# The weight-block sums for v's products: when their DRAM-to-DRAM transfers are asked for

## The chip, the core and the metric

The kernel runs on one core of a Trainium2 chip. A core has a matrix engine (TensorE, "PE" in the profile), a vector engine (VectorE, "DVE"), a scalar engine (ScalarE, "ACT"), GpSimd ("POOL"), SyncE ("SP"), and 16 DMA engines that all queues share. The metric is the device time of one execution in microseconds; a kernel's time is the median of its runs.

## What is computed

One decoder layer on x of shape (1, 512, 2048), in float32:

```python
h = _rmsnorm(x, g_pre)
proj = h @ w_in                                   # (512 x 2048) @ (2048 x 7168)
q, k, v, z_att, u, g_glu, z_conv = jnp.split(proj, IN_SPLITS, axis=-1)
y_att = _stick_breaking_attention(q, k, v) * jax.nn.silu(z_att)
y_conv = _conformer_conv(u, g_glu, conv_w, conv_b, ln_g, ln_b, w_pw2, b_pw2) * jax.nn.silu(z_conv)
y = jnp.concatenate([y_att, y_conv], axis=-1) @ w_out
return x + _rmsnorm(y, g_post)
```

Each of the seven parts of `proj` has 1024 columns. This case is about the part v, and about the parts u, q and k that are computed just before it.

## The kernel before

**Products.** Every float32 operand is split into a high and a low part, and a product takes three matrix multiplies (high by high, high by low, low by high). A weight block of 1 MB is loaded by one DMA that SP issues into a tile `r_...` (pool `raws`, two buffers); ACT makes the high part `h_...` from it (line 99, pool `his`, two buffers) and DVE the low part `l_...` (line 100, pool `los`, two buffers). So the load of one block waits until the split of the block two before it is through, and a high part is written only when PE has done the products with the high part two before it.

**The order of the work.** The opening (from line 1189) computes the first half of the gate g in sixteen blocks `(kg, m)` while x is loaded, transposed and normalised. Then the list `steps` is run (from line 1229). A step has one loaded weight block and two units of products; `n_v` = 6 steps come first (u, q and k for the first pair of heads: u0, u1, q0, q1, k0, k1 for short), and their units have 24 multiplies each. Then come the fourteen steps of `values()`, two for each of the seven products that v is made of, in the order 1, 2, 5, 6, 3, 7, 4. Their units have 12 multiplies each, so a block is needed twice as often there. They are called v10, v11, v20, v21, v50, v51 and so on: product, then half. Their tile is `r_v`, with the same name for all fourteen. PE's order is the program's; the order on DVE and ACT is fixed when the kernel is compiled. DVE also works through 240 steps of the convolution (`acc`, lines 396 and 401), placed between the others.

**The sums.** v is computed by a scheme with seven block products in place of eight; the weight operands of the products 5, 6, 7 and 4 are sums of blocks of `w_in`. These sums are made in DRAM by DMAs alone: for each sum and each of its two halves, a base block is copied into a DRAM tile `vs` (line 506), and then another block is added to it by an accumulating DMA (line 502). `plan_sums` (line 492) lists them in this order: copies of 5 (two halves), accumulations of 5, copies of 6 (from the finished sum 5, so `vs` to `vs`), accumulations of 6, copies of 7, accumulations of 7, copies of 4 (from sum 6), accumulations of 4. That is sixteen transfers of 1 MB each, all issued by GpSimd in this order. GpSimd also issues two loads of the opening and clears a small border tile `hg` (line 392).

**When a sum is asked for.** `sum_next` (line 514) takes the next transfer from the list and makes it wait for the last multiply that has been written down so far:

```python
def sum_next(todo):
    if todo:
        tc.add_manual_dep(
            todo.popleft()().ins, latest[0].name,
            ...
```

It is called with `v_sumq` at the end of each opening block from number 5 on (line 1197), and then after every unit of every step (line 1258), until the list is empty. Eleven transfers fall into the opening's blocks 5 to 15, and the other five wait for the first five units. A transfer that builds on another also waits for that one to land, and GpSimd issues in order. The halves of the sums are loaded by line 612 when the steps v50, v51, v60, v61, v70, v71, v40 and v41 come near.

The sums for the output projection (`ws`, `sumq`) are another list, asked for from step 18 on.

## Time and profile before

| | |
|---|---|
| median of 3 runs | 870.81 us (869.97 to 870.85) |
| the profiled execution: whole time | 871.51 us |
| the profiled execution: span from the first to the last instruction | 869.8 us |
| TensorE clock granted over it | 0.997 |
| DVE busy | 631.0 us (73%) |
| ACT busy | 395.3 us (45%) |
| GpSimd's DMA queue (q0): moved, share of the 16 engines' span | 52.43 MB, 26.1% |
| SP's DMA queue (q1): moved, share of the 16 engines' span | 110.12 MB, 37.3% |

The page of the profile gives shares over the whole span. What a transfer does to the work around it has to be read from narrow windows: the timeline of an engine gives start and length of each instruction, in brackets how long the engine sat idle before it and what ended that. The DMA share of a window is the mean busy share of the 16 DMA engines; it can go a little over 1, since packets overlap and are counted where they start.

### The profile page before, as it was taken

How to read it: one execution, taken by the hardware profiler on the slowest of the kernel's cores; microseconds unless marked ns; L12 is line 12 of the kernel's file. 1: busy time of each engine (PE TensorE's matmuls, PEld its weight loads, DVE VectorE, ACT ScalarE, POOL GpSimd, SP SyncE). 2: the span in 40 equal slices, each digit the busy share in tenths (PEclk: the TensorE clock that was granted, in tenths of full speed). 3: DMA queues.
4: the chain of work that ended last, by engine and by line, in shares of the span. 5: the costliest groups of instructions: out<-in, count | busy, mean ns of one | idle time of the engine just before them, and what ended most of it. 6: DMA issues, size and time to landing. Idle time of an engine off the chain costs nothing.

```text
span 869.8 us, 9834 instructions
## 1 busy us (share of the span) xinstructions
PE 855.0 (98%) x3894; PEld 710.0 (82%) x3894; DVE 631.0 (73%) x773; ACT 395.3 (45%) x452; POOL 124.5 (14%) x154
## 2 busy tenths in 40 slices
PE   9999998999999999999999999999999999999995
PEld 7888787888888888888888888888888888888884
DVE  4798799986797979879696984245643776458775
ACT  5785124644443544243422545235722346455542
POOL 0221100001202132203111323031001000000031
PEclk9999999999999999999999999999999999999998
DMA  8899964568578455874488547862232346556783
GB/s 324 250 272 283 281 158 160 185 207 302 173 181 174 165 193 145 179 189 165 145 192 165 176 157 183 175 162 97 93 101 97 98 154 233 194 194 250 289 279 101
DMA packets 87046, 163.58 MB, mean 188 GB/s; under 512 B 3014, under 2 KB 52434, under 8 KB 83224
## 3 DMA queue, kind: packets, MB, share of 16 engines
q1 hardware_dynamic: 69824, 110.12, 37.3%
q0 software_dynamic: 16864, 52.43, 26.1%
q8 instruction: 30, 0.49, 0.2%
q10 hardware_dynamic: 312, 0.40, 0.1%
q14 instruction: 16, 0.13, 0.0%
HBM read 158.75 MB, written 54.53 MB: 245 GB/s over the span
## 4 chain that ended last, share of the span: by engine, by line
PE 80%; DVE 10%; DMA 6%; ACT 2%; issue 1%; POOL 0%; DVEq 0%; ACTq 0%; POOLq 0%
PE za L342 3%; PE zc L342 3%; PE za L344 3%; PE a L940 3%; PE zc L344 3%; PE za L343 3%; PE a L942 3%; PE zc L343 3%; PE a L941 3%; DVE acc L401 3%; DVE l_v L100 3%; DMA r_k<-in_w_in_dram 3%; PE k L342 3%; PE q L344 3%; PE q L342 3%; PE u L344 3%
## 5 line engine op out<-in xcount | busy, mean ns | idle before, releaser
L401 DVE SCALAR_TENSOR_TENSOR acc<-hg,vec,acc 128x512 f32<-128x512 f32 x240 | 182.2, 759 | 6.8
L100 DVE TENSOR_TENSOR l_w<-r_w,h_w 128x2048 fp32r<-128x2048 f32 x28 | 64.1, 2291 | 41.9 <-ACT h_w L99 41.9
L99 ACT ACTIVATE h_w<-r_w 128x2048 fp32r<-128x2048 f32 x28 | 53.5, 1915 | 42.1 <-DMA r_w<-ws 11.8
L344 PE MATMUL k<-h_hi,l_k 128*128 128x512 f32 x128 | 50.1, 391 | 1.1 <-DVE l_k L100 1.1
L342 PE MATMUL u<-h_hi,h_u 128*128 128x512 f32 x128 | 50.3, 393 | 0.0
L342 PE MATMUL q<-h_hi,h_q 128*128 128x512 f32 x128 | 50.1, 392 | 0.0
L342 PE MATMUL k<-h_hi,h_k 128*128 128x512 f32 x128 | 50.0, 391 | 0.0
L342 PE MATMUL za<-h_hi,h_za 128*128 128x512 f32 x128 | 50.0, 390 | 0.0
L342 PE MATMUL zc<-h_hi,h_zc 128*128 128x512 f32 x128 | 49.9, 390 | 0.0
L344 PE MATMUL u<-h_hi,l_u 128*128 128x512 f32 x128 | 49.9, 390 | 0.0
L344 PE MATMUL q<-h_hi,l_q 128*128 128x512 f32 x128 | 49.9, 390 | 0.0
L344 PE MATMUL za<-h_hi,l_za 128*128 128x512 f32 x128 | 49.8, 389 | 0.0
L344 PE MATMUL zc<-h_hi,l_zc 128*128 128x512 f32 x128 | 49.8, 389 | 0.0
L343 PE MATMUL u<-h_lo,h_u 128*128 128x512 f32 x128 | 49.8, 389 | 0.0
L343 PE MATMUL k<-h_lo,h_k 128*128 128x512 f32 x128 | 49.8, 389 | 0.0
L343 PE MATMUL za<-h_lo,h_za 128*128 128x512 f32 x128 | 49.8, 389 | 0.0
L343 PE MATMUL q<-h_lo,h_q 128*128 128x512 f32 x128 | 49.8, 389 | 0.0
L343 PE MATMUL zc<-h_lo,h_zc 128*128 128x512 f32 x128 | 49.8, 389 | 0.0
L940 PE MATMUL a<-h_w,f_hi 128*128 128x512 f32 x128 | 49.8, 389 | 0.0
L941 PE MATMUL a<-l_w,f_hi 128*128 128x512 f32 x128 | 49.8, 389 | 0.0
L942 PE MATMUL a<-h_w,f_lo 128*128 128x512 f32 x128 | 49.8, 389 | 0.0
L671 POOL TENSOR_SCALAR_AFFINE_SELECT t<-t 128x128 f32<-128x128 f32 x64 | 35.7, 635 | 81.1 <-DVE t L694 48.2
(339 smaller groups left out, 2136.7 us busy)
## 6 DMA issues: line engine op xcount, KB each, us to landing
ws<-in_w_out_dram POOLq DMA_DIRECT2D x24, 1024.0 KB, 9.3
r_w<-ws SPq DMA_DIRECT2D x16, 1024.0 KB
vs<-in_w_in_dram POOLq DMA_DIRECT2D x12, 1024.0 KB, 12.9
r_w<-in_w_out_dram SPq DMA_DIRECT2D x12, 1024.0 KB
r_u<-in_w_in_dram SPq DMA_DIRECT2D x8, 1024.0 KB
r_q<-in_w_in_dram SPq DMA_DIRECT2D x8, 1024.0 KB
r_k<-in_w_in_dram SPq DMA_DIRECT2D x8, 1024.0 KB
r_v<-vs SPq DMA_DIRECT2D x8, 1024.0 KB
```

The lines of the kernel that those rows point to most:

```text
L99: nc.scalar.activation(hi, src, AF.Copy)
L100: nc.vector.tensor_tensor(out=lo, in0=src, in1=f32(hi), op=ALU.subtract)
L342: nc.tensor.matmul(ps, wh, ah, start=first, stop=False)
L343: nc.tensor.matmul(ps, wh, al, start=False, stop=False)
L344: latest[0] = nc.tensor.matmul(ps, wl, ah, start=False, stop=last).ins
L401: bgq.append(lambda j=j: nc.vector.scalar_tensor_tensor(out=acc, in0=hg[:, j : j + S], scalar=vec[:, ct, j : j + 1], in1=acc, op0=ALU.mult ...
L671: nc.gpsimd.affine_select(out=blk, in_=blk, compare_op=ALU.is_gt, fill=0.0, base=0, pattern=[[-1, P]], channel_multiplier=1,)
L940: nc.tensor.matmul(ps, fh[:, kk, ts], hi[:, k, :], start=st, stop=False, skip_group_check=True)
L941: nc.tensor.matmul(ps, fh[:, kk, ts], lo[:, k, :], start=False, stop=False, skip_group_check=True)
L942: nc.tensor.matmul(ps, fl[:, kk, ts], hi[:, k, :], start=False, stop=en, skip_group_check=True)
```

## The change

The first hunk moves the start of the requests in the opening from block 5 to block 10, so that six transfers (the copies and accumulations of sum 5, the copies of sum 6) are asked for there. The second hunk counts the units of the steps; after a unit a transfer is asked for only if the count isn't a multiple of three. The remaining ten transfers are so tied to the units 1, 2, 4, 5, 7, 8, 10, 11, 13 and 14, counted from the first unit of u0.

```diff
@@ -1194,7 +1194,7 @@
                 f()
             if n + 1 < len(blocks):
                 keeps[n + 1]()
-            if n >= 5:
+            if n >= 10:
                 sum_next(v_sumq)
...
+    units_done = 0
     for n, step in enumerate(steps):
...
         for unit in step.units:
             unit(w)
-            sum_next(v_sumq)
+            units_done += 1
+            if units_done % 3:
+                sum_next(v_sumq)
```

The list, its order, the transfers themselves and everything else stay as they are.

## The prediction

> **What bounds the kernel now.** First the page's busy times, then the waits of PE, which say whether anything but PE's own work is left.

> ```profile
> PE 855.0 (98%) x3894; PEld 710.0 (82%) x3894; DVE 631.0 (73%) x773; ACT 395.3 (45%) x452; POOL 124.5 (14%) x154
> ```

> ```profile
> PE va L635 <- DVE l_v L100: 2.4, 1, 2.4
> PE k L344 <- DVE l_k L100: 1.1, 1, 1.1
> PE va L634 <- ACT v_a L596: 0.4, 1, 0.4
> ```

> PE works for 98% of the span, and its own waits are few: 2.4 us at a block of v, 1.1 us at k, 0.4 us at a later block of v. The change can touch 1.1 + 2.4 = 3.5 us of this and no more: a faster delivery of weights can't shorten PE's own products. What it can add has no such limit.

> Where the two waits come from, in the chain of waits (start, length, what; in order of time):

> ```profile
> 58.12 19.88 DMA r_q<-in_w_in_dram
> 78.11 1.93 ACT h_q L99
> 80.06 2.30 DVE l_q L100
> 82.38 21.91 DMA r_k<-in_w_in_dram
> 104.39 1.93 ACT h_k L99
> 106.34 2.29 DVE l_k L100
> ```

> Two 1 MB loads in a row take 19.9 and 21.9 us; k0's low part is finished at 108.63. PE starts on it at once (the 1.1 us). DVE has been standing, and from here on it is late:

> ```profile
> 80.06 2.29 DVE L100 TENSOR_TENSOR l_q<-r_q,h_q 128x2048 fp32r<-128x2048 f32 x1 [3.88 <-ACT h_q L99]
> 92.50 9.40 DVE L401 SCALAR_TENSOR_TENSOR acc<-hg,vec,acc 128x512 f32<-128x512 f32 x12
> 106.34 2.29 DVE L100 TENSOR_TENSOR l_k<-r_k,h_k 128x2048 fp32r<-128x2048 f32 x1 [4.44 <-ACT h_k L99]
> 129.03 0.68 DVE L100 TENSOR_TENSOR k_lo<-k,k_hi 128x512 fp32r<-128x512 f32 x1
> 136.38 2.28 DVE L100 TENSOR_TENSOR l_v<-r_v,h_v 128x2048 fp32r<-128x2048 f32 x1
> 147.43 2.28 DVE L100 TENSOR_TENSOR l_v<-r_v,h_v 128x2048 fp32r<-128x2048 f32 x1
> ```

> It idles 3.88 us for q0 and 4.44 us for k0. No idle time stands before the later rows: DVE works without a gap from 106.34, so l_v of v11 (136.38) comes when its turn comes, ends at 138.66, and PE takes it up at 138.72:

> ```profile
> 68.73 0.50 PE L342 MATMUL u<-h_hi,h_u 128*128 128x512 f32 x1
> 130.48 0.39 PE L634 MATMUL va<-h_v,h_hi 128*128 128x512 f32 x1
> 138.72 0.50 PE L635 MATMUL va<-l_v,h_hi 128*128 128x512 f32 x1 [2.41 <-DVE l_v L100]
> 149.78 0.49 PE L635 MATMUL vc<-l_v,h_hi 128*128 128x512 f32 x1
> ```

> The last row is the first use of l_v of v21, which DVE ended at 147.43 + 2.28 = 149.71: the next block comes just in time, with no slack and no wait.

> Why the loads are slow: the DMA share of stretches (last two columns: share, GB/s).

> ```profile
> 61.00:101.00 40.00, 39.96 (x188) 32.88 (x186) 35.76 (x59) 15.35 (x20) 6.10 (x7) 1.00 1.07 285
> 121.00:200.00 79.00, 76.59 (x337) 62.66 (x336) 73.57 (x81) 39.06 (x40) 1.00 (x3) 1.00 0.51 174
> ```

> From 61 to 101 us the engines are full (1.07); after 121, when the sums have landed, they are half idle (0.51). That is what the change levels out. It matters that the half-idle stretch is the one where blocks are needed every 5.5 us instead of every 11.

> **The change, part by part.**

> *No instruction is removed or added on PE, DVE, ACT or SP.* The sixteen transfers stay; GpSimd only waits for other multiplies. Queued behind a waiting transfer on GpSimd are later transfers and the clearing of `hg` for u's next pair, which comes after the fourteen steps of v: free.

> *The new times.* From 68.73 (unit 2) to 130.48 (unit 13, v10) are 61.75 us, less the wait of 1.11, over eleven units: 5.51 us each. Without the waits, unit 4 ends at 85.3, 5 at 90.8, 7 at 101.8, 8 at 107.3, 10 at 118.3, 11 at 123.8, 12 at 129.4; units 13 and 14 are half as long and end at 132.1 and 134.8.

> The opening:

> ```profile
> 28.88 0.72 POOL L506 DMA_DIRECT2D vs<-in_w_in_dram  x1 [5.26 <-PE gn L478]
> 32.09 0.71 POOL L506 DMA_DIRECT2D vs<-in_w_in_dram  x1 [2.50 <-PE gn L478]
> DMA to landing us min/median/max: 5.5/5.6/5.7
> DMA to landing us min/median/max: 8.9/9.0/9.0
> L612 SPq DMA_DIRECT2D r_v<-vs x8: 319/330/349, 143.7 to 192.9; - x8
> ```

> Blocks are 3.2 us apart, so block 10 asks at 28.88 + 5 x 3.21 = 45 us. A copy alone lands in 5.6 us, an accumulation alone (here two of `ws`) in 9.0. Copies of 5 go out at 45 and 48, accumulations at 52 and 55; the copies of 6 wait for these to land (about 61 and 68), the accumulations of 6 for the copies (about 70 and 75), then units rule: copies of 7 at 85 and 91, accumulations of 7 at 102 and 107, copies of 4 at 118 and 124, **accumulations of 4 at 132.4 and 135.1**, landed by about 152. The eight halves are loaded from 143.7 to 192.9 us (last row) in the order 5, 6, 7, 4; sum 5 is there at 68, and by 143.7 all but sum 4, whose loads are the last two: no sum comes too late.

> *What goes: up to 3.5 us.* In flight while q0 loads (asked for at 58.12, which is set by DVE, not by a load) are two accumulations that are nearly done by 66 and two copies; before, two accumulations that had just started and three copies. I estimate q0 by 71 instead of 78. Its high part needs u0's buffer, free at unit 2's end (74.2), so the 3.9 us of idle DVE go. k0 is then asked for at about 78.5. From 72 to 100 the engines have two accumulations to move, three loads and two copies.

> ```profile
> q0 software_dynamic: 199, 0.41, 72.8%
> q1 hardware_dynamic: 174, 0.36, 35.5%
> q1 hardware_dynamic: 7, 0.01, 0.6%
> q1 hardware_dynamic: 481, 0.97, 94.2%
> ```

> Of the first two rows (112 to 115 us) an accumulation's packet takes 0.728 x 3 us x 16 / 199 = 0.176 us of one engine; 512 packets of 2 KB make 5.6 us of all sixteen. A load alone moves 481 packets in 3 us (last row), so 3.2 us. Two of the one, three of the other and two copies (under 5.6 each, I take 3) are 27 us of 28, with k0 ahead of the last ones: landed at about 92 to 95 instead of 104.3. It isn't wanted before its `h_k` buffer is free (unit 6, 96.3) and DVE's 12 convolution steps are over. So DVE's idle 4.44 us go as well. PE's 1.1 us go. For the 2.4 us, DVE must be ahead by 1.1 + 2.4 = 3.5 us at v11. What could hold it:

> ```profile
> 121.25 1.92 ACT L99 ACTIVATE h_v<-r_v 128x2048 fp32r<-128x2048 f32 x1 [9.97 <-DMA r_v<-in_w_in_dram]
> 125.24 0.60 ACT L99 ACTIVATE k_hi<-k 128x512 fp32r<-128x512 f32 x1 [2.08 <-PE k L344]
> 130.46 1.92 ACT L99 ACTIVATE h_v<-r_v 128x2048 fp32r<-128x2048 f32 x1 [4.61 <-PE k L343]
> 144.31 1.92 ACT L99 ACTIVATE h_v<-r_v 128x2048 fp32r<-128x2048 f32 x1 [2.13 <-PE va L636]
> ```

> k_hi (125.24) waits for unit 11, at 123.8 then and 124.9 before; right behind it comes k_lo on DVE, at 129.03 before, so DVE can be ahead by 4 us here. h_v of v11 (130.46) waits for PE, 1.1 us earlier. l_v of v11 then starts at about 132.2 and ends at 134.4; PE wants it at 135.0. Both waits go: **-3.5 us**. If only x of DVE's lead is kept, x goes (bounds 0 and -3.5).

> *What comes: v21's load among the accumulations of 4.* v21 is asked for when l_v of v11 frees its buffer: at 138.69 before, 134.4 then; the accumulations go out at 132.4 and 135.1, on both sides of it. Until now the loads of this stage met none. With both waits gone PE wants l_v of v21 at 149.78 - 3.51 = 146.3; behind the landing come 1.92 (h_v) and 2.28 (l_v), with 0.1 between. If v21 lands at L, the net change is L + 4.3 - 149.7 = **L - 145.4 us**, and never below -3.5 (L up to 141.9). Now L:

> ```profile
> 108.66 0.37 SPq L612 DMA_DIRECT2D r_v<-in_w_in_dram  x1
> 138.69 0.37 SPq L612 DMA_DIRECT2D r_v<-in_w_in_dram  x1
> 101.43 1.18 POOL L502 DMA_DIRECT2D vs<-in_w_in_dram  x1 [16.18 <-DMA vs<-vs]
> 104.33 1.16 POOL L502 DMA_DIRECT2D vs<-in_w_in_dram  x1 [1.72 <-DMA vs<-vs]
> DMA to landing us min/median/max: 11.7/14.2/16.6
> ```

> - From below: v21 before, without company, was asked for at 138.69 and used at 144.31, 5.6 us later, and ACT waited for PE there, not for it. L = 134.4 + 5.6 = 140.0: no new wait, net -3.5.
> - The nearest row: v10, the same kind of load, asked for at 108.66 beside two accumulations (101.43, 104.33) and landed when ACT took it at 121.25: 12.6 us. L = 147.0, net +1.6. Built from packets it is the same: hardly one has moved by 111 (7 packets in the 107 to 111 row), then 174 in 3 us; 512 take 8.8 us, so 2.9 + 8.8 and the tail.
> - From above: both accumulations go wholly ahead. The later of two landed 16.6 us after its issue: 135.1 + 16.6 = 151.7, net +6.3.

> I take 12.6 us, the row that is the same transfer in the same company. Afterwards nothing catches up: v50's load queues right behind and is needed 5.5 us later, and from then on PE stands as close behind DVE as before.

> Sum: -1.1 - 2.4 + 5.1 = **+1.6 us**. The profiled execution, 869.8 of span and 1.7 around it, becomes 871.5 + 1.6 = 873.1; its time is 0.7 above the median of the runs, so the forecast is 870.8 + 1.6 = **872.4 us**.

> [...]

> **The rivals.**

> - [...] 14%.
> - *v21 is hidden*: it gets through before the accumulations are dense, L below 141.9, full gain of 3.5: **867.3**. For it: 2 us pass between the issue of an accumulation and its flow. Against: the second is already queued. 22%.
> - *Slower: the accumulations win.* Place: v21, on the DMA queues from 132 to 152 us; price up to +6.3 (**877**); it decides from L = 147.1, as net +1.7 is the border. For it: the load at 82.38 took 21.9 us. 14%.
> - *The change does not do what it says*: q0 and k0 are no faster, for there are four accumulations and four copies between 52 and 101 as before; the waits stay, and v21, asked for late, meets less: about **870.8**. Against: q0 and k0 are met by other ones, older or lighter. 8%.

> The forecast has 42%, net +0.3 to +3.3.

> **How the numbers follow.** A measurement of this kernel can tell about 0.2% (1.7 us) from nothing. Faster: the second rival, 22%. Within 0.2%: the first and the last, and half the forecast's band, 43%. Slower: the other half and the third, 35%. The range reaches from the full gain, 867.3, to 875.8 (L = 150.4), leaving out the far end of the third rival and little below. The forecast's own band is 871.1 to 874.1.

> **What would show it.** Right: no wait of PE at k; q0 and k0 landing 7 to 10 us earlier; DVE without its two gaps; a new wait at v21 (vc, lines 634 and 635) of about 5 us, with the accumulations of 4 in flight over it. Wrong: no wait there (second rival); v21 asked for at another time than 134, which means that DVE's order or lead came out differently; a wait at v11 that stays.

## The result and the profile after

The changed kernel is **slower by 0.48%**: a median of 874.84 us (874.03 to 876.01, six runs) against 871.33 us (869.97 to 873.05, six runs) for the kernel before in the same comparison, a ratio of 1.0048 with a 95% interval of 1.0030 to 1.0065. The profiled execution took 874.75 us with a span of 873.0; before it took 871.51 with a span of 869.8. The forecast was 872.4, so the sign was right and the size, 1.6 us against 3.2 in the two profiled executions and 3.5 between the medians, was half of what came: 874.84 lies above the forecast's own band (871.1 to 874.1) and inside its range (up to 875.8).

The page's busy times after the change:

```profile
PE 856.5 (98%) x3894; PEld 712.0 (82%) x3894; DVE 631.1 (72%) x773; ACT 395.3 (45%) x452; POOL 124.6 (14%) x154
```

The instructions are as many as before. PE is busy for 1.5 us more (856.5 against 855.0) with the same multiplies, so some of them took longer; the span is 3.2 us longer, so the other 1.7 us are idle time. The waits of PE say where the idle time is:

```profile
PE vc L634 <- ACT h_v L99: 3.7, 1, 3.7
PE vc L635 <- DVE l_v L100: 1.8, 1, 1.8
```

The waits at k (1.1), at v11 (2.4) and at a later block (0.4) are gone. One new place has come, the first two multiplies of v21, with 3.7 and 1.8 us. The chain of waits around it (start, length, what):

```profile
131.18 2.30 DVE l_v L100
133.49 13.08 DMA r_v<-in_w_in_dram
146.67 1.92 ACT h_v L99
148.62 2.30 DVE l_v L100
150.96 0.79 PE vc L635
```

The low part of v11 ends at 133.46 and frees the buffer; v21 is asked for at once, lands at 146.57 after 13.08 us, and goes through ACT and DVE with PE standing still. GpSimd's issues in that stretch, on its timeline, and the landing line of the view of the sums' tile `vs` from 131 to 152 us:

```profile
131.61 1.19 POOL L502 DMA_DIRECT2D vs<-in_w_in_dram  x1 [7.64 <-PE va L636]
134.33 1.16 POOL L502 DMA_DIRECT2D vs<-in_w_in_dram  x1 [1.53 <-PE va L636]
```

```profile
DMA to landing us min/median/max: 10.1/13.4/16.7
```

The accumulations of sum 4 are issued at 131.61 and 134.33, on both sides of v21's request at 133.49, and land after 10.1 and 16.7 us, the second one at 151.0. The queues show how v21 got through between them: from 133.5 to 137.5 us (first two rows: packets, MB, share of the 16 engines' span; q0 is GpSimd's, q1 is SP's) and from 138 to 144 us (last two):

```profile
q0 software_dynamic: 297, 0.61, 104.6%
q1 hardware_dynamic: 3, 0.01, 0.5%
```

```profile
q0 software_dynamic: 395, 0.78, 69.6%
q1 hardware_dynamic: 392, 0.80, 39.8%
```

For 4 us the load moves three packets against 297; then the two queues move about as many packets, 395 against 392. This is the late start that the row of v10 had shown in the kernel before. About 1 us of it is there without company too: v21 in the kernel before, asked for at 138.69 with no accumulation in flight, moved its first packet between 139.70 and 139.75, 1.0 us after its request; here it took 3.8.

The other side of the ledger, on the timelines of ACT and of DVE (in brackets: idle time before, and what ended it):

```profile
74.05 1.92 ACT L99 ACTIVATE h_q<-r_q 128x2048 fp32r<-128x2048 f32 x1 [0.51 <-PE u L343]
97.90 1.92 ACT L99 ACTIVATE h_k<-r_k 128x2048 fp32r<-128x2048 f32 x1 [10.99 <-DMA r_k<-in_w_in_dram]
```

```profile
76.00 2.29 DVE L100 TENSOR_TENSOR l_q<-r_q,h_q 128x2048 fp32r<-128x2048 f32 x1
99.85 2.29 DVE L100 TENSOR_TENSOR l_k<-r_k,h_k 128x2048 fp32r<-128x2048 f32 x1 [1.29 <-ACT h_k L99]
131.18 2.28 DVE L100 TENSOR_TENSOR l_v<-r_v,h_v 128x2048 fp32r<-128x2048 f32 x1
148.62 2.29 DVE L100 TENSOR_TENSOR l_v<-r_v,h_v 128x2048 fp32r<-128x2048 f32 x1 [6.30 <-ACT h_v L99]
```

DVE's gap of 3.88 us at q0 is gone (the row at 76.00 has no bracket), and that at k0 has shrunk from 4.44 to 1.29. ACT takes q0 at 74.05 not when it lands but when PE frees the buffer. DVE reaches l_v of v11 at 131.18 instead of 136.38. So the early half of the change does what its diff says. What it doesn't explain is in PE's timeline behind the new wait:

```profile
148.64 0.50 PE L634 MATMUL vc<-h_v,h_hi 128*128 128x512 f32 x1 [3.73 <-ACT h_v L99]
150.96 0.79 PE L635 MATMUL vc<-l_v,h_hi 128*128 128x512 f32 x1 [1.82 <-DVE l_v L100]
151.55 0.63 PE L636 MATMUL vc<-h_v,h_lo 128*128 128x512 f32 x1
151.98 0.63 PE L634 MATMUL vc<-h_v,h_hi 128*128 128x512 f32 x1
...
156.67 0.40 PE L636 MATMUL vc<-h_v,h_lo 128*128 128x512 f32 x1
156.91 0.40 PE L634 MATMUL vc<-h_v,h_hi 128*128 128x512 f32 x1
```

Between 151.55 and 156.67 a multiply starts every 0.43 us and takes 0.63; then they are back at 0.23 and 0.40. The clock granted to PE is the last column but two in the view by windows:

```profile
146.00:148.60 2.60, 0.00 (x0) 0.00 (x0) 0.00 (x0) 1.93 (x2) 0.00 (x0) 1.00 1.05 343
148.70:150.90 2.20, 0.44 (x1) 0.12 (x1) 2.20 (x2) 1.64 (x4) 0.00 (x0) 0.76 0.72 174
151.00:156.00 5.00, 5.00 (x12) 3.94 (x13) 5.00 (x6) 2.62 (x3) 0.00 (x0) 0.50 0.59 210
156.90:160.00 3.10, 3.10 (x15) 2.54 (x14) 1.89 (x4) 0.81 (x1) 0.00 (x0) 1.00 0.88 307
```

The clock is 1.00 while PE waits for the high part, falls in the middle of the second wait (0.76 over that window), stands at **0.50 over the window from 151 to 156**, and is 1.00 again in the last one. Comparing the start of every multiply with the same multiply before gives the whole ledger, after minus before: -0.33 from the opening, -1.57 once k's wait is gone, -1.90 (a stall of 0.33 at k1 gone, too short for the list of waits), -4.63 at v11, +1.19 at the first multiply with l_v of v21 (149.78 before, 150.96 now), +3.84 at the end of the slow stretch, and about +3.2 from the next small wait (0.4 us, gone) to the end. What went and the two new waits together come to +1.2; the slow clock adds 2.65, more than twice that.

### The profile page after: what moved, and what is told of

It reads as the page before. It is cut to its first block, busy times and chain, and to the rows that moved or that the text cites. A ratio compares the mean times of both kernels' runs of the same rounds, so it can differ in the third digit from the quotient of the medians.

```text
span 873.0 us, 9834 instructions
## 1 busy us (share of the span) xinstructions
PE 856.5 (98%) x3894; PEld 712.0 (82%) x3894; DVE 631.1 (72%) x773; ACT 395.3 (45%) x452; POOL 124.6 (14%) x154
## 4 chain that ended last, share of the span: by engine, by line
PE 93%; DVE 3%; DMA 1%; ACT 1%; issue 0%; POOL 0%; DVEq 0%; ACTq 0%; POOLq 0%
PE u L342 3%; PE u L344 3%; PE za L342 3%; PE q L342 3%; PE q L344 3%; PE u L343 3%; PE zc L342 3%; PE za L344 3%; PE a L940 3%; PE zc L343 3%; PE zc L344 3%; PE q L343 3%; PE za L343 3%; PE a L941 3%; PE a L942 3%; PE k L342 3%
## 5 line engine op out<-in xcount | busy, mean ns | idle before, releaser
L401 DVE SCALAR_TENSOR_TENSOR acc<-hg,vec,acc 128x512 f32<-128x512 f32 x240 | 182.2, 759 | 6.8
L100 DVE TENSOR_TENSOR l_w<-r_w,h_w 128x2048 fp32r<-128x2048 f32 x28 | 64.1, 2291 | 42.1 <-ACT h_w L99 42.1
L99 ACT ACTIVATE h_w<-r_w 128x2048 fp32r<-128x2048 f32 x28 | 53.5, 1915 | 43.7 <-DMA r_w<-ws 16.1
L342 PE MATMUL u<-h_hi,h_u 128*128 128x512 f32 x128 | 50.3, 393 | 0.0
L342 PE MATMUL q<-h_hi,h_q 128*128 128x512 f32 x128 | 50.1, 392 | 0.0
L342 PE MATMUL k<-h_hi,h_k 128*128 128x512 f32 x128 | 50.0, 391 | 0.0
L342 PE MATMUL za<-h_hi,h_za 128*128 128x512 f32 x128 | 50.0, 390 | 0.0
L342 PE MATMUL zc<-h_hi,h_zc 128*128 128x512 f32 x128 | 49.9, 390 | 0.0
L344 PE MATMUL u<-h_hi,l_u 128*128 128x512 f32 x128 | 49.9, 390 | 0.0
L344 PE MATMUL q<-h_hi,l_q 128*128 128x512 f32 x128 | 49.9, 390 | 0.0
L344 PE MATMUL zc<-h_hi,l_zc 128*128 128x512 f32 x128 | 49.8, 389 | 0.0
L344 PE MATMUL za<-h_hi,l_za 128*128 128x512 f32 x128 | 49.8, 389 | 0.0
L343 PE MATMUL u<-h_lo,h_u 128*128 128x512 f32 x128 | 49.8, 389 | 0.0
L343 PE MATMUL za<-h_lo,h_za 128*128 128x512 f32 x128 | 49.8, 389 | 0.0
L344 PE MATMUL k<-h_hi,l_k 128*128 128x512 f32 x128 | 49.8, 389 | 0.0
L343 PE MATMUL q<-h_lo,h_q 128*128 128x512 f32 x128 | 49.8, 389 | 0.0
L343 PE MATMUL k<-h_lo,h_k 128*128 128x512 f32 x128 | 49.8, 389 | 0.0
L343 PE MATMUL zc<-h_lo,h_zc 128*128 128x512 f32 x128 | 49.8, 389 | 0.0
```

What stands on the lines that cost most here:

```text
L99: nc.scalar.activation(hi, src, AF.Copy)
L100: nc.vector.tensor_tensor(out=lo, in0=src, in1=f32(hi), op=ALU.subtract)
L342: nc.tensor.matmul(ps, wh, ah, start=first, stop=False)
L343: nc.tensor.matmul(ps, wh, al, start=False, stop=False)
L344: latest[0] = nc.tensor.matmul(ps, wl, ah, start=False, stop=last).ins
L401: bgq.append(lambda j=j: nc.vector.scalar_tensor_tensor(out=acc, in0=hg[:, j : j + S], scalar=vec[:, ct, j : j + 1], in1=acc, op0=ALU.mult ...
```

## The experiments

The theory after the result: the late start (first hunk) is a gain of about 3 us; the thinning (second hunk), on top of it, brings the last two accumulations beside v21's load; PE's wait there costs 5.5 us; and because of the wait, not because of the transfers, the clock falls and costs 2.65 more. The rivals: that the thinning is what unloads the opening, that v21 is late for another reason than these two accumulations, and that the slow multiplies come from the traffic of the DMAs.

### The first hunk alone

```diff
-            if n >= 5:
+            if n >= 10:
...
             unit(w)
             sum_next(v_sumq)
```

> The first hunk alone: six transfers in the opening, then one after every unit, so that the accumulations of 4 are asked for at units 9 and 10 (113 and 118 us) and have landed by about 130. Theory (the loss is v21's load meeting the accumulations of 4): no wait of PE at k, v11 or v21, all of the gain and none of the loss, 3.5 to 4.3 us below before (ratio 0.995 to 0.996). Rival (the late start in the opening costs time by itself, since the same transfers are pressed into less time): q0 or k0 land as late as before or later, waits at k and v11 of 3.5 us or more, at or above before (1.000 to 1.005).

Measured: 867.7 us (866.2 to 869.36, twelve runs), a ratio of 0.9967 (0.9956 to 0.9978). The waits of PE from 60 to 205 us:

```profile
PE vc L635 <- DVE l_v L100: 1.5, 2, 1.2
```

Two waits of 1.5 us together are all that is left; none had been expected, and the gain is a little smaller than said (0.995 to 0.996). The accumulations of sum 4 are issued at 118.7 and 120.9, some 13 us earlier than in the change. So the gain belongs to the late start alone; asking less densely isn't needed for it.

### The second hunk alone

```diff
             if n >= 5:
                 sum_next(v_sumq)
...
-            sum_next(v_sumq)
+            units_done += 1
+            if units_done % 3:
+                sum_next(v_sumq)
```

> The second hunk alone: eleven transfers in the opening from block 5 on, the other five at units 1, 2, 4, 5 and 7; the accumulations of 4 are asked for by 102 us. Theory: no wait at v21 (the last landing is before 125 us); the queues are full between 58 and 88 us as before, so the waits at k and v11 stay in part: 0 to 3 us below before (0.9965 to 1.000). Rival (asking after two units in three is what costs): slower than before by 2 us or more (1.002 or more).

Measured: 871.3 us (869.84 to 872.38, twelve runs), a ratio of 1.0007 (0.9994 to 1.0019): no change. So the second hunk by itself costs nothing measurable; put on top of the first one it costs 874.84 - 867.7 = 7.1 us, since only behind the late start does it move the last two accumulations to v21. Its wait, and then the clock around it by windows (the first is the wait, the second the multiplies behind it):

```profile
PE va L635 <- DVE l_v L100: 2.4, 1, 2.4
```

```profile
135.00:137.40 2.40, 0.05 (x1) 0.00 (x0) 2.40 (x3) 1.77 (x1) 0.00 (x0) 1.00 0.00 0
137.50:140.90 3.40, 3.40 (x9) 2.65 (x10) 3.33 (x5) 0.00 (x0) 0.00 (x0) 0.53 0.67 196
```

Here k's wait has gone and v11's wait of 2.4 us has stayed. It is the same wait as before, 2.43 us against 2.41, and this time the clock falls to 0.53 behind it, with nine multiplies in 3.4 us. From the first of them at 137.48 to the first fast one at 141.24 are 3.76 us; the same nine took 2.21 in the kernel before (from 138.72), so one such stretch costs about 1.6 us. In the kernel before, the same two windows read:

```profile
136.40:138.60 2.20, 0.00 (x0) 0.00 (x0) 2.20 (x3) 1.63 (x1) 0.00 (x0) 1.00 0.00 0
138.80:142.00 3.20, 3.20 (x14) 2.62 (x15) 3.13 (x5) 0.41 (x1) 0.00 (x0) 1.00 0.66 189
```

There the clock stays at 1.00, and 14 multiplies take 3.2 us. The DMA share behind the wait is the same (0.66 and 0.67), so the traffic isn't what slows PE here; and the length of the wait alone (2.41 and 2.43 us) isn't either; what decides between the two isn't shown (last section).

### Without the last two accumulations

```diff
     v_sum, v_sumq = plan_sums("vs", (5, 6, 7, 4), 1, v_w)
+    for _ in range(2):
+        v_sumq.pop()
```

> The changed kernel without the two accumulations of sum 4 (sum 4 lacks one of its two blocks, so that part of v is another one). Theory: v21 lands within 6 us of being asked for, PE waits nowhere between 60 and 200 us by more than 0.5 us, and the clock stays at 1.00: 3.5 to 4.5 us below before (0.995 to 0.996), some 8 us below the changed kernel. Rival (the loss has another cause, such as the transfers of 7 or DVE's order): within 2 us of the changed kernel (1.003 or more).

This kernel leaves out the second block of sum 4. Measured: 866.23 us (865.89 to 866.98, six runs), a ratio of 0.9953 (0.9937 to 0.9969). From 60 to 205 us PE waits once:

```profile
PE va L637 <- DVE l_v L100: 0.4, 1, 0.4
```

With the rest of the change in place, these two transfers cost 874.84 - 866.23 = 8.6 us; there was nothing else at v21. It is also what a placing of these two that costs nothing would reach, with the other fourteen as in the change.

### The wait filled with multiplies

Twenty-four multiplies whose result nobody reads stand on PE between v20 and v21, so that PE works while v21 is on its way.

```diff
+            if (q, kg, i) == (2, 1, 0):
+                fill = trp.tile([P, S], F32, tag="tr", name="fill")
+                for _ in range(24):
+                    nc.tensor.matmul(fill, mean_w, h_hi[0][:, 0, :], start=True, stop=True)
             ps = v_ps[q, i]
```

> The changed kernel with 24 multiplies more, whose result nothing reads, put on PE between v20 and v21, where it waits 5.5 us: 24 x 0.2275 = 5.5 us of work in place of idle time. Theory (PE's clock falls to half because PE has stood still, and that costs another 2.8 us): the granted clock is 1.00 from 150 to 158 us, v21's multiplies follow each other at 0.23 us and not at 0.43, and the time is 2.3 to 3 us below the changed kernel (1.0015 against 1.0048 of before). Rival (the slow multiplies from 151 to 157 us come from the transfers or from something else in that stretch): still 0.43 us, and the time of the changed kernel or a little more.

Measured: 880.06 us (878.93 to 880.34, five runs), a ratio of 1.0109 (1.0091 to 1.0127). As a whole this run missed its expectation (1.0015): the added work changed the order that the compiler gave to ACT and DVE behind v21, and waits of 1.12 and 3.33 us appeared further on. The place that it was made for can still be read. The same window as after the change, and then the second slow stretch:

```profile
151.00:156.00 5.00, 4.91 (x22) 4.07 (x23) 5.00 (x7) 2.71 (x3) 0.00 (x0) 1.00 0.58 210
163.70:166.90 3.20, 0.00 (x0) 0.00 (x0) 3.17 (x4) 3.20 (x5) 0.00 (x0) 1.00 0.00 0
167.60:170.60 3.00, 3.00 (x8) 2.34 (x7) 2.89 (x5) 0.24 (x1) 0.00 (x0) 0.50 0.84 309
```

From 151 to 156 us the engines move the same (share 0.58, 210 GB/s, against 0.59 and 210), yet the clock is 1.00 and 22 multiplies run where 12 did. Where PE really stood still, from 163.7 to 166.9, the clock is 0.50 behind it. So here the fall follows PE's idle time (3.33 us), and the transfers don't make it.

### The last two accumulations later, in two ways

Both keep the change and move only the last two. The one at units 21 and 22:

```diff
-            if units_done % 3:
+            if units_done % 3 and units_done < 13 or units_done in (21, 22):
```

> The changed kernel with the two accumulations of sum 4 asked for at units 21 and 22 (v50) instead of 13 and 14, so at about 152 and 155 us, where the loads are those of finished sums (packets of 8 KB). Theory (the wait stands where a load meets these two, and a load with larger packets gets more bytes for its turn): no wait at v21, and a smaller one, 0 to 3 us, at one of v60 to v30; 0.5 to 4 us below before (0.9955 to 0.9995). Rival (v21 waits for another reason): its wait of 5 us stays and another comes on top: 1.005 or more. Rival (a load of any packet size loses the same): a wait of 5 us moves to v60 or v61: 1.002 to 1.006.

(On the larger packets: loads of finished sums moved 1.24 MB in 167 packets from 184 to 190 us in the kernel before; from 144 to 147 us after the change, with packets of v21 and of v50, SP's queue moved 0.60 MB in 160 packets beside 0.32 MB in 155 of GpSimd's.)

Measured: 872.05 us (871.1 to 873.57, twelve runs), a ratio of 1.0018 (1.0005 to 1.0030), slower than was expected (0.9955 to 0.9995). v21's wait is gone, but its kind has moved along. On the timelines of ACT and of PE:

```profile
164.42 1.92 ACT L99 ACTIVATE h_v<-r_v 128x2048 fp32r<-128x2048 f32 x1 [3.00 <-DMA r_v<-vs]
172.58 1.92 ACT L99 ACTIVATE h_v<-r_v 128x2048 fp32r<-128x2048 f32 x1 [5.77 <-DMA r_v<-in_w_in_dram]
```

```profile
168.72 0.50 PE L635 MATMUL va<-l_v,vf_01h 128*128 128x512 f32 x1 [1.82 <-DVE l_v L100]
176.87 0.50 PE L635 MATMUL vb<-l_v,vf_00h 128*128 128x512 f32 x1 [0.82 <-DVE l_v L100]
```

v61 and v30 are now the loads that ACT waits for, 3.00 and 5.77 us, and PE waits 1.82 and 0.82 us behind them. These waits are within the 0 to 3 us that were expected, but behind the one of 1.82 us the clock is 0.50 again, and that had not been. The other at units 14 and 15, one unit later than in the change:

```diff
-            if units_done % 3:
+            if units_done % 3 and units_done < 13 or units_done in (14, 15):
```

> The changed kernel with the two accumulations of sum 4 asked for at units 14 and 15 instead of 13 and 14, so 2.7 us later: at 134.3 and 137.1 us, just behind v21's load (133.5) and not on both sides of it. Theory (most of the 13.1 us is that a load asked for while an accumulation flows gets no turn for some 4 us, and then one turn in two): v21's load starts at once, most of it is through before the accumulations flow, it takes 6 to 8 us and PE doesn't wait at v21 for more than 0.5 us; v50's load (asked for at 138.5) now comes into their flow and takes 9 to 10 us, with 1 to 3 us of waiting at v50, with or without a short stretch at half the clock: 0.3 to 3 us below before (0.9965 to 0.9997). Rival (what counts is only that both overlap): v21's load still takes 11 us or more, 3 us or more of waiting at v21, 1.001 or more.

Measured: 868.61 us (867.61 to 868.85, eleven runs), a ratio of 0.9981 (0.9972 to 0.9990), its time as expected and the wait at v50 a little shorter than said (1 to 3 us). The waits of PE from 60 to 206 us, and ACT's row of v50:

```profile
PE vb L635 <- DVE l_v L100: 0.9, 1, 0.9
PE va L635 <- DVE l_v L100: 0.2, 1, 0.2
```

```profile
147.03 1.92 ACT L99 ACTIVATE h_v<-r_v 128x2048 fp32r<-128x2048 f32 x1 [4.19 <-DMA r_v<-vs]
```

Here v21 is asked for at 133.39, before the first accumulation (134.23), and ACT takes it at 139.40 without waiting for it. v50, asked for at 138.43, takes 8.6 us and costs PE 0.9. **One unit of delay, and 6 us of the 874.84 are gone**: the load asked for ahead of both accumulations wasn't held up (v21 was there within 6.0 us), and the one behind them cost PE only 0.9.

### The last two as plain copies

In `plan_sums`, the accumulations of sum 4 become copies of the same size without an addition (sum 4 then holds one block and not the sum of two):

```diff
+            if accumulate and name == "vs" and q == 4:
+                return nc.gpsimd.dma_start(made[q, p, kg], block(*more, p, kg))
```

> The changed kernel with the last two transfers as plain copies of the same blocks in place of accumulations (sum 4 then holds one block and not the sum of two), asked for at the same units 13 and 14. They have half as many packets (256 of 4 KB in place of 512 of 2 KB), and a copy is 2.9 us of the engines in place of 5.6. Theory (v21 waits for the engine time of the two): v21's load takes 8 to 10 us in place of 13.1, the wait at v21 is 0 to 2 us, no half clock: 2 to 4 us below before (0.995 to 0.998). Rival (any transfer of GpSimd beside the load holds it back alike): still 12 us or more, 1.003 or more.

Measured: 868.71 us (868.06 to 870.99, twelve runs), a ratio of 0.9981 (0.9971 to 0.9992). ACT's row of v21 and PE's two rows behind it:

```profile
143.09 1.92 ACT L99 ACTIVATE h_v<-r_v 128x2048 fp32r<-128x2048 f32 x1 [5.80 <-DMA r_v<-in_w_in_dram]
```

```profile
145.06 0.49 PE L636 MATMUL vc<-h_v,h_hi 128*128 128x512 f32 x1 [0.24 <-ACT h_v L99]
147.39 0.50 PE L637 MATMUL vc<-l_v,h_hi 128*128 128x512 f32 x1 [1.83 <-DVE l_v L100]
```

v21 is there at 143.09; asked for at about 133.4, as in the two runs next to this one (133.49 after the change, 133.39 at units 14 and 15), it took some 9.7 us instead of 13.1. PE waits 0.24 and 1.83 us, and the clock stays at 1.00 (147.5 to 152 us). The price of the meeting went down with the engine time of what was met: in the kernel before, 303 packets of copies took 96.0% of the 16 engines from 31.5 to 35 us, 0.18 us of one engine each and about as much as an accumulation's 0.176, but a packet of a copy holds 4 KB (35 packets, 0.14 MB, from 28 to 31 us) and one of an accumulation 2 (199 packets, 0.41 MB, from 112 to 115). So the number of packets was halved along with the engine time, and no run separates the two. 3.4 us on the load were 6.1 us on the kernel.

### Other starts in the opening, with a request after every unit

```diff
-            if n >= 5:
+            if n >= 8:
```

> The first hunk with 8 in place of 10, then one transfer after every unit: everything 6 us earlier than in the kernel with the first hunk alone, which still waited 1.5 us before v21 since v20's load met the accumulations of 4. Theory: that wait goes and none comes at k or v11: 1 us below the first hunk alone (0.9945 to 0.9965). Rival (q0 and k0 meet more again): waits at k or v11 come back, 0.997 to 1.000.

Measured: 868.34 us (867.39 to 870.76, twelve runs), a ratio of 0.9971 (0.9960 to 0.9982).

```diff
-            if n >= 5:
+            if n >= 7:
```

> The same with 7. Theory: between the one with 8 and before; if k0's load stays ahead of its need, as with 8 (0.9945 to 0.9965). Rival: k0 lands after 98 us and DVE stands before l_k for 2 us or more, part of v11's wait comes back: 0.997 to 1.000.

Measured: 867.55 us (866.53 to 868.23, six runs), a ratio of 0.9959 (0.9945 to 0.9973). The waits of PE from 60 to 206 us, first with the start at 8, then at 7:

```profile
PE va L635 <- DVE l_v L100: 2.4, 1, 2.4
PE k L344 <- DVE l_k L100: 1.0, 1, 1.0
```

```profile
PE va L635 <- DVE l_v L100: 1.8, 1, 1.8
```

At 8 the two old waits are nearly whole again (2.4 and 1.0), at 7 one of 1.8 is left, at 10 (above) 1.5 in all. But the profiled execution with 8 took 870.76 us, the slowest of its twelve and 2.4 above their median, so its waits say little of the other eleven. Neither theory came out: with 8 the waits were to go, and 7 was to lie between 8 and before. The three medians lie within 0.8 us of each other and their intervals overlap, so no start among 7, 8 and 10 is shown to be best. Each of them is 2.7 to 3.5 us faster than the kernel before, and faster than the change by more. **The version to keep is the first hunk alone, or a start at block 7**; without the last two accumulations it was 0.9953.

## Why the prediction came out as it did

**"What goes: up to 3.5 us": right.** PE's waits at k and at v11 went, and with the stall of 0.33 at k1 and 0.33 from the opening PE stood 4.6 us ahead at v11, so "3.5 us of this and no more" was 1.1 too little. On the way, q0 came as said (it waits for its buffer, at 74.05 against 74.2). k0 was asked for at 78.32 (said: 78.5) but landed at 97.90, not at 92 to 95: three loads, two accumulations and two copies took 3 us more of the engines than my sum of their parts. That left DVE a gap of 1.29 us and cost nothing, since the lead was enough for both waits.

**"The new times": right.** The accumulations of 4 were said to go out at 132.4 and 135.1 and went at 131.61 and 134.33; l_v of v11 was said to end at 134.4 and ended at 133.46.

**"What comes: v21's load among the accumulations of 4": right in mechanism and in the load's price.** It took 13.08 us; the row of v10 gave 12.6. That the two are so close owes something to luck: v10 was asked for behind both accumulations and v21 between them, and 0.8 us ahead of both, in the run at units 14 and 15, the same load took no more than 6.0. The request came 0.9 us before the time said, which took back the longer load. With L = 146.57 the formula L - 145.4 gives +1.2, and the measured lag at the first multiply with l_v was +1.19. Of the three bounds, the nearest row was the right one: the same kind of load in the same company. Once the load flowed, the two queues moved about as many packets (395 against 392). Over the first 4 us the load got no such share (3 against 297); where its packets stood by then, no run shows.

**"Sum: -1.1 - 2.4 + 5.1": this is the step that failed.** It prices PE's new wait at its length and lets PE go on at full speed behind it ("from then on PE stands as close behind DVE as before"). The missing term is the clock: thirteen multiplies at half speed, +2.65 us, of which the later waits that vanish give about 0.6 back. The waits, 3.73 + 1.82, and 0.27 for the end of the single multiply between them, which no next one overlaps, turn -4.63 into +1.19, as the forecast's formula has it; +2.65 - 0.6 make it +3.2. The one trace of the kernel before couldn't teach this with its wait of 2.41 us, since its clock stayed at 1.00, and I took that one case for the rule. Its other executions hint at the fall: of the 67 that ran beside the experiments, 23 were granted 0.994 or 0.995 over the span (median 871.6 us) and the others 0.996 to 0.998 (870.3), and the profiled execution of the second hunk alone, with its one slow stretch, was granted 0.995 against 0.997 in the kernel before. With the term the forecast would have been some 872.4 + 2.65 - 0.6 = 874.4.

**The rivals.** "v21 is hidden" would have needed the load before the accumulations in the queues; one unit of delay does that (868.61). "The change does not do what it says" fell with the waits at k and v11. "Slower: the accumulations win" gave a time near the measured one for a cause that isn't there: it decides from L = 147.1, and L was 146.57. The direction came out of the likeliest case, but its size came from a term that no case had.

## What to carry to other kernels

A background transfer is cheap or dear by the stage it meets, not by how evenly it is spread: here the opening's crowd cost 3 us and two accumulations in the stage with a block every 5.5 us cost 8.6, so place the last of them against the due times of the loads, and see that the urgent load is asked for first. An idle time of TensorE can cost more than its own length: of the eight traces here with waits from 1.77 to 3.73 us, four had the clock at half behind them, which cost 1.6 us with the second hunk alone and 2.65 after the change. To look at an edit with two hunks, run each alone and compare both with the pair: here one hunk alone gained 3.4 us, the other alone changed nothing, and the second on top of the first lost 7.1. The loss is in their meeting, which neither hunk shows alone.

## What was not expected of the hardware

| trace | wait of PE (us) | window behind it (us) | clock in it |
|---|---|---|---|
| the change | 3.73, then 1.82 | 151.0 to 156.0 | 0.50 |
| filled wait | 3.33 | 167.6 to 170.6 | 0.50 |
| second hunk alone | 2.43 | 137.5 to 140.9 | 0.53 |
| units 21 and 22 | 1.82 | 170.0 to 172.0 | 0.50 |
| before | 2.41 | 138.8 to 142.0 | 1.00 |
| start at 8 | 2.39 | 138.5 to 142.0 | 1.00 |
| copies | 1.83 | 147.5 to 152.0 | 1.00 |
| start at 7 | 1.77 | 136.1 to 140.0 | 1.00 |

Two waits of nearly the same length, at units 21 and 22 (1.82 us, ended at 168.72) and with the copies (1.83, ended at 147.39), have these rows behind them:

```profile
168.00:170.00 2.00, 1.28 (x5) 1.10 (x6) 2.00 (x4) 0.00 (x0) 0.00 (x0) 0.94 1.09 261
170.00:172.00 2.00, 2.00 (x6) 1.54 (x6) 1.67 (x3) 0.00 (x0) 0.00 (x0) 0.50 1.07 289
147.50:152.00 4.50, 4.50 (x20) 3.73 (x21) 4.50 (x6) 1.87 (x3) 0.00 (x0) 1.00 0.64 233
```

The slow multiplies did not always come at once: at units 21 and 22 the first that takes 0.63 us starts at 169.76, 1.0 us after the wait has ended, and the last at 172.31; in the filled wait they start from 167.65 to 170.21, with the second hunk alone from 137.88 to 140.44, and after the change the clock is 0.50 from 149.9 to 156.6 us, with PE idle in it until 150.96, the rest of the wait for l_v. So length alone doesn't sort the waits: 1.82 and 2.43 us had half the clock behind them, 1.83 and 2.41 did not. What decides, and what brings the clock back, isn't shown: no run moved such a wait and kept its length.

**A load asked for while an accumulation flowed moved its first packet late.** By the DMA view in narrow windows, v21 after the change, asked for at 133.49, has no packet by 137.30 and its first by 137.31, so it took 3.8 us; v10 in the kernel before, asked for at 108.66 beside two accumulations, has none by 112.22 and three by 112.25, so 3.6; v21 in the kernel before, without company, took the 1.0 us given above. So some 2.6 to 2.8 us of the late start came with the accumulations. What was met mattered too: v21 took 13.1 us beside two accumulations and some 9.7 beside two copies. By what they held the load up stays open.
